# Query projection of the next head group written tile by tile between the attention heads of this group

## The chip, the cores and the metric

The kernel runs on one core of a Trainium2 chip. The metric is device time in microseconds (us) of one launch. The engines of a core work in parallel, each on its own list of instructions in order: TensorE (PE for matmuls, PEld for its weight loads), VectorE (DVE), ScalarE (ACT), GpSimd (POOL) and SyncE (SP), which issues most loads. Matmul results land in PSUM, in banks of 512 columns of 128 partitions.

## What is computed

A two-layer decoder trunk over 512 tokens of width 1024: a matrix-memory (mLSTM) layer, then a sliding-window attention layer. Each layer ends with a squared-ReLU MLP and a gated input embedding. The change lies in the attention of the second layer:

```
q = partial_rope((x @ w_q + b_q).reshape(B, S, A_Q_HEADS, A_HEAD_DIM), pos)
scores = einsum('bnqkgd,bnskd->bnkgqs', q, kb) * (A_HEAD_DIM ** -0.5)
scores = where(valid, scores, -inf)            # window of 128 tokens
m = maximum(max(scores, -1), sink)
e = exp(scores - m)
probs = e / (sum(e, -1) + exp(sink - m))
out = einsum('bnkgqs,bnskd->bnqkgd', probs, vb).reshape(B, S, D_MODEL)
return out @ w_o + b_o
```

There are 16 query heads in 4 groups; the 4 heads of a group share one key and value head. Tokens are worked in 4 tiles of 128.

## The kernel before

Every matrix product is made of three float32r matmuls (`mm3`, L87 to L90): each operand is split into a high part (a rounded copy, made by ScalarE) and a low part (the difference, made by VectorE). Weights come by DMA into `wraw`, ScalarE casts them to `whi` (L76), VectorE subtracts to `wlo` (L77); there are six buffers of each of the two.

The attention stage works on pairs of a head group `gi` (0 to 3) and a token tile `t` (0 to 3), with two functions.

`q_group(gi, t, w)` projects the queries of one group and tile: 24 matmuls of 128x256 into half a PSUM bank `mm` (two such banks; tiles 0 and 1 share one, tiles 2 and 3 the other). VectorE adds the bias and so empties the half bank (`q`, L839); POOL rotates (L786 to L789); TensorE transposes twice into the one bank `tp` (L843); ScalarE and VectorE write high and low parts into `QS` (L848, L849).

`attend(gi, t)` does the attention of the four heads of that group and tile. TensorE computes the scores in two halves of four matmuls, each half in one of three `sc` banks (L860, L861). VectorE masks (L865), takes the maximum (L866) and forms the negative maximum `anm` (L871) and the sink term `es` (L873); ScalarE takes four exponentials with their sums (L879) and that of the sink (L874); VectorE adds, inverts and scales the probabilities `pr` (L881 to L883). TensorE transposes them into a `pt` bank (L887, four transposes); ScalarE makes the high part `ah` (L891), VectorE the low part `al` (L892); for t > 0 POOL masks both into `bh` and `bl` (L899). Then 6 (t = 0) or 12 value matmuls go into another `pt` bank (two in all), and the result replaces the queries in `QS` (L910, L911).

Group 0's queries are projected ahead of the loop over the groups. The loop (L919 to L924) loads the next group's query weights, and runs `attend` and `q_group` over the four tiles. After it comes the last group's `attend`, with parts of the output projection (`wo_part`, L926 to L930) of the first two tiles between (L938). The engines' lists are not in the source's order: a scheduler sorts the instructions of the whole program by their place in the source and by its own estimate of when each could run, engine by engine. A list is then fixed; on the chip each engine follows its own.

Of the kernel before, what the change touches and what calls it, by code (L numbers as in the profile page):

```python
# [21 lines left out]
NT = S // P  # L22
# [23 lines left out]
def yoco_kernel(ctx: ExitStack, tc: tile.TileContext, A: dict, out: bass.AP):  # L46
# [18 lines left out]
    def mm_bank():  # L65
        return bank("mm")

    def tp_bank():
        return bank("tp")

    def f32(t):
        return t.bitcast(F32)
# [6 lines left out]
    def load_w(src, n, eng=V):  # L79
        raw = wpool.tile([P, 1024], F32, tag="raw", name="wraw", bufs=3)  # L80
        hi = wpool.tile([P, 1024], F32R, tag="whi", name="whi", bufs=6)
        lo = wpool.tile([P, 1024], F32R, tag="wlo", name="wlo", bufs=6)
        nc.sync.dma_start(raw[:, :n], src)
        split(raw[:, :n], n, hi[:, :n], lo[:, :n], eng)
        return hi, lo

    def mm3(o, lh, ll, rh, rl, start, stop):  # L87
        PE.matmul(o, lh, rh, start=start, stop=False)  # L88
        PE.matmul(o, lh, rl, start=False, stop=False)  # L89
        PE.matmul(o, ll, rh, start=False, stop=stop)  # L90
# [18 lines left out]
    def tsl(t):  # L109
        return slice(t * P, (t + 1) * P)  # L110
# [669 lines left out]
    def rope(x, t, nh, eng):  # L780
        tr = x[:, :, 0:ROPE].rearrange("p h (a j) -> p h a j", a=2)
        ca = cos[:, t, :].unsqueeze(1).unsqueeze(1).broadcast_to([P, nh, 2, HALF])
        sa = sin[:, t, :].unsqueeze(1).unsqueeze(1).broadcast_to([P, nh, 2, HALF])
        ta = pb.tile([P, KVH, 2, HALF], F32, tag="ta", name="ta", bufs=2)[:, :nh]
        tb = pb.tile([P, KVH, 2, HALF], F32, tag="tb", name="tb", bufs=2)[:, :nh]
        eng.tensor_mul(ta, tr, ca)  # L786
        eng.tensor_mul(tb, tr, sa)
        eng.tensor_sub(tr[:, :, 0, :], ta[:, :, 0, :], tb[:, :, 1, :])
        eng.tensor_add(tr[:, :, 1, :], ta[:, :, 1, :], tb[:, :, 0, :])  # L789
# [9 lines left out]
    w = [load_w(A["w_kv"][0, c], 1024) for c in range(4)]  # L799
# [30 lines left out]
    def q_group(gi, t, w):  # L830
        if t % 2 == 0:
            qbank[0] = mm_bank()
        ps = qbank[0][:, (t % 2) * 256:(t % 2 + 1) * 256]
        for k in range(KD):
            wh, wl = w[k // 4]
            sl = slice((k % 4) * 256, (k % 4 + 1) * 256)
            mm3(ps, XH[:, k, tsl(t)], XL[:, k, tsl(t)], wh[:, sl], wl[:, sl], k == 0, k == KD - 1)
        q = pb.tile([P, 256], F32, tag="qr", name="q", bufs=2)
        V.tensor_add(q, ps, bq[:, gi * 256:(gi + 1) * 256])  # L839
        rope(q.rearrange("p (h d) -> p h d", d=HD), t, KVH, GP)  # L840
        pt = tp_bank()
        for pr in range(2):
            PE.transpose(pt[:, tsl(pr)], q[:, tsl(pr)], ident)  # L843
        pv = pt[:, :256].rearrange("p (a s) -> p a s", a=2)
        for par in range(2):
            own, other = slice(par * HD, (par + 1) * HD), slice((1 - par) * HD, (2 - par) * HD)
            hs = slice(4 * gi + par, 4 * gi + par + 3, 2)
            ACT.copy(QS[own, hs, tsl(t)], pv[own])  # L848
            V.tensor_sub(QS[other, hs, tsl(t)], pv[own], f32(QS)[own, hs, tsl(t)])  # L849
# [63 lines left out]
    def load_q(gi):  # L913
        return [load_w(A["w_q"][gi, c], 1024) for c in range(2)]

    w = load_q(0)
    for t in range(NT):
        q_group(0, t, w)
    for gi in range(KVH - 1):  # L919
        w = load_q(gi + 1)  # L920
        for t in range(NT):
            attend(gi, t)
        for t in range(NT):
            q_group(gi + 1, t, w)  # L924

    def wo_part(ps, t, w, k0, k1):  # L926
        for k in range(k0, k1):
# [4 lines left out]
    w = [load_w(A["w_o"][0, c], 1024) for c in range(4)]  # L932
# [16 lines left out]
    for half in range(2):  # L949
        if half == 1:  # L950
            w = [load_w(A["w_o"][1, c], 1024) for c in range(4)]
# [90 lines left out]
```

## Time and profile before

| | us |
|---|---|
| runs of the kernel before (3) | 1203.20, 1203.77, 1205.82; median 1203.77 |
| the profiled execution | 1205.69 |
| its span, first to last instruction | 1204.0 |
| TensorE busy with matmuls | 1178.7 |
| VectorE busy | 879.0 |
| ScalarE busy | 587.5 |

The attention stage lies at 657 to 760 us of the span. A row of the trace gives the start of an instruction, its duration, engine, line in the kernel, operation, output and inputs, and in brackets how long the engine had been idle before and what released it. Matmuls overlap: each of 128x256 shows 0.28 us, while the next one starts 0.12 us later, so the distance of two starts tells what one costs.

### The profile page before, as it was taken

The numbers are of one execution on the slowest core, as the hardware profiler recorded it, in microseconds if no ns is written. First come the engines' busy times: TensorE is split into PE (matmuls) and PEld (weight loads), VectorE is DVE, ScalarE is ACT, GpSimd is POOL, SyncE is SP. The second block draws the span as 40 slices with busy tenths as digits, with TensorE's granted clock in tenths as the row PEclk, the third lists the DMA queues.
The fourth block names the chain that finished last, engine by engine and source line by source line (L and its number), as shares of the span: only waits on it lengthen the run. The fifth ranks groups of instructions, "written<-read, shape, count | busy, mean of one in ns | idle before, by whom it ended". The sixth has DMA issues, their size and how long they took to land. (4 is left out here: it accounts for less than half of the span.)

```text
span 1204.0 us, 15649 instructions
## 1 busy us (share of the span) xinstructions
PE 1178.7 (98%) x5918; PEld 1001.0 (83%) x5918; DVE 879.0 (73%) x1451; ACT 587.5 (49%) x1016; POOL 95.8 (8%) x189
## 2 busy tenths in 40 slices
PE   8999999999999999999999999989999999999998
PEld 7899998888888888888788998779888888888877
DVE  6555556878488589599786888596847848959974
ACT  4645552565464463464344655346645536346431
POOL 1011020100000000001201342110000000000100
PEclk9999999999999999999999999999999999999999
DMA  7322226214505306215252211361350440631511
GB/s 247 101 80 69 84 89 260 90 35 128 153 1 175 105 19 194 68 53 160 76 180 101 71 37 36 122 228 36 94 169 18 140 141 1 191 89 36 155 56 52
DMA packets 35707, 124.54 MB, mean 103 GB/s; under 512 B 4064, under 2 KB 4592, under 8 KB 35632
## 3 DMA queue, kind: packets, MB, share of 16 engines
q1 hardware_dynamic: 33552, 116.46, 30.4%
q0 software_dynamic: 2080, 7.09, 1.8%
q8 instruction: 46, 0.75, 0.2%
q14 instruction: 29, 0.24, 0.1%
HBM read 119.34 MB, written 4.19 MB: 103 GB/s over the span
## 5 line engine op out<-in xcount | busy, mean ns | idle before, releaser
L77 DVE TENSOR_TENSOR wlo<-wraw,whi 128x1024 fp32r<-128x1024 f32 (+1 forms) x168 | 204.1, 1218 | 125.2 <-ACT whi L76 124.2
L76 ACT CAST whi<-wraw 128x1024 fp32r<-128x1024 f32 (+1 forms) x168 | 173.7, 1037 | 239.6 <-PE mm L90 132.8
L88 PE MATMUL mm<-XH,whi 128*128 128x512 f32 (+1 forms) x640 | 235.1, 370 | 1.2 <-ACT ot L230 1.0
L89 PE MATMUL mm<-XL,whi 128*128 128x512 f32 (+1 forms) x640 | 235.9, 369 | 0.0
L90 PE MATMUL mm<-XH,wlo 128*128 128x512 f32 (+1 forms) x640 | 235.7, 369 | 0.0
L88 PE MATMUL mm<-whi,XH 128*128 128x512 f32 (+2 forms) x424 | 146.0, 345 | 3.9 <-DVE q L839 2.2
L89 PE MATMUL mm<-wlo,XH 128*128 128x512 f32 (+2 forms) x424 | 145.3, 343 | 0.0
L90 PE MATMUL mm<-whi,XL 128*128 128x512 f32 (+2 forms) x424 | 144.7, 343 | 0.0
L88 PEld LDWEIGHTS mm<-XH,whi 128*128 128x128 f32 x640 | 120.4, 189 | 21.8 <-ACT ot L230 1.4
L90 PEld LDWEIGHTS mm<-XH,wlo 128*128 128x128 f32 x640 | 121.1, 189 | 20.0
L89 PEld LDWEIGHTS mm<-XL,whi 128*128 128x128 f32 x640 | 121.1, 189 | 19.6
L76 ACT CAST whi<-rb 128x1024 fp32r<-128x1024 f32 x80 | 84.0, 1050 | 101.0 <-PE mm L89 56.4
L77 DVE TENSOR_TENSOR wlo<-rb,whi 128x1024 fp32r<-128x1024 f32 x80 | 97.4, 1221 | 38.9 <-ACT whi L76 38.9
L88 PEld LDWEIGHTS mm<-whi,XH 128*128 128x128 f32 x424 | 79.9, 189 | 13.0 <-DVE q L839 3.9
L89 PEld LDWEIGHTS mm<-wlo,XH 128*128 128x128 f32 x424 | 80.1, 189 | 7.7 <-issue 1.5
L90 PEld LDWEIGHTS mm<-whi,XL 128*128 128x128 f32 x424 | 80.1, 189 | 6.5 <-issue 0.8
L89 PE MATMUL mm<-wlo,S23h 128*128 128x512 f32 x128 | 50.7, 396 | 0.0
L89 PE MATMUL mm<-wlo,S4Ah 128*128 128x512 f32 x128 | 50.6, 395 | 0.0
L88 PE MATMUL mm<-whi,S23h 128*128 128x512 f32 x128 | 50.6, 395 | 0.0
L88 PE MATMUL mm<-whi,S4Ah 128*128 128x512 f32 x128 | 50.6, 395 | 0.0
L90 PE MATMUL mm<-whi,S4Al 128*128 128x512 f32 x128 | 50.3, 395 | 0.0
L633 DVE TENSOR_TENSOR res<-res,mm 128x512 f32<-128x512 f32 x72 | 48.6, 682 | 1.5 <-PE mm L90 1.0
(356 smaller groups left out, 2233.2 us busy)
## 6 DMA issues: line engine op xcount, KB each, us to landing
wraw<-in_w_up_dram SPq DMA_DIRECT2D x64, 512.0 KB, 3.9
rb<-in_w_down_dram SPq DMA_DIRECT2D x48, 512.0 KB, 4.4
wraw<-in_w_down_dram SPq DMA_DIRECT2D x16, 512.0 KB, 3.5
wraw<-in_w_gate_dram SPq DMA_DIRECT2D x16, 512.0 KB, 3.8
wraw<-in_w_vo_dram SPq DMA_DIRECT2D x19, 412.0 KB, 3.5
wraw<-in_w_qk_dram SPq DMA_DIRECT2D x8, 512.0 KB, 3.7
wraw<-in_w_out_dram SPq DMA_DIRECT2D x8, 512.0 KB, 3.9
wraw<-in_w_q_dram SPq DMA_DIRECT2D x8, 512.0 KB, 3.9
```

The costliest lines, as they stand in the source:

```text
L76: ACT.copy(hi, raw)
L77: eng.tensor_sub(lo, raw, f32(hi))
L88: PE.matmul(o, lh, rh, start=start, stop=False)
L89: PE.matmul(o, lh, rl, start=False, stop=False)
L90: PE.matmul(o, ll, rh, start=False, stop=stop)
L633: V.tensor_add(r[:, h], r[:, h], bank)
```

## The change

In the loop over the groups, `q_group(gi + 1, t, w)` is written immediately before `attend(gi, t)`, tile by tile, instead of in a loop of its own after the four tiles. Neither function is changed.

```diff
     for gi in range(KVH - 1):
         w = load_q(gi + 1)
         for t in range(NT):
+            q_group(gi + 1, t, w)
             attend(gi, t)
-        for t in range(NT):
-            q_group(gi + 1, t, w)
```

What the scheduler makes of it is seen in the engines' lists. Three places follow. The numbers in names tell buffers apart and differ between the two kernels.

Place 1: VectorE's list while the scores of group 0, tile 1 are worked on. Before, `sc_5777` is the second score half of that tile, `sc_5827` the first one of tile 2, `q_6004` the queries of group 1, tile 1.

```order
L883 TENSOR_TENSOR pr_5742<-pr_5742,sm_5743 128x512
L865 COPY_PREDICATED sc_5777<-mask_328,sc_5777 128x2x128
L866 TENSOR_REDUCE smax_5769<-sc_5777 128x2
L839 TENSOR_TENSOR q_6004<-mm_5940,bq_5268 128x256
L865 COPY_PREDICATED sc_5827<-mask_328,sc_5827 128x2x128
```

In the changed kernel the same four are `sc_5856`, `sc_5946`, `q_5833` and the probabilities `pr_5782`.

```order
L883 TENSOR_TENSOR pr_5782<-pr_5782,sm_5783 128x512
L865 COPY_PREDICATED sc_5856<-mask_328,sc_5856 128x2x128
L839 TENSOR_TENSOR q_5833<-mm_5722,bq_5268 128x256
L866 TENSOR_REDUCE smax_5848<-sc_5856 128x2
L865 COPY_PREDICATED sc_5946<-mask_328,sc_5946 128x2x128
```

The add of the queries has moved ahead of the reduction. A little later on the same list, behind the scaling of the next probabilities, the add for group 1, tile 2 stood like this before:

```order
L883 TENSOR_TENSOR pr_5789<-pr_5789,sm_5790 128x512
L865 COPY_PREDICATED sc_5834<-mask_328,sc_5834 128x2x128
L866 TENSOR_REDUCE smax_5826<-sc_5834 128x2
L911 TENSOR_TENSOR QS_5326<-pt_5760,QS_5326 128x2x128
L871 SCALAR_TENSOR_TENSOR anm_5841<-smax_5826,nsink_5270 128x4
L865 COPY_PREDICATED sc_5884<-mask_328,sc_5884 128x2x128
L839 TENSOR_TENSOR q_6044<-mm_6019,bq_5268 128x256
```

and now stands like this, with two steps between instead of five:

```order
L883 TENSOR_TENSOR pr_5868<-pr_5868,sm_5869 128x512
L911 TENSOR_TENSOR QS_5326<-pt_5800,QS_5326 128x2x128
L865 COPY_PREDICATED sc_5953<-mask_328,sc_5953 128x2x128
L839 TENSOR_TENSOR q_5930<-mm_5905,bq_5268 128x256
L849 TENSOR_TENSOR QS_5326<-tp_5755,QS_5326 64x2x128
```

Place 2: TensorE's list at the transposes of the probabilities of group 0, tile 2. Before, these are `pt_5855`; behind them come half a score half and the 24 matmuls of one projection (`mm_6407`, group 2, tile 2), and then the first value matmul, into `pt_5868`.

```order
L887 MATMUL pt_5855<-ident_66,pr_5846 128x128 x4
L860 MATMUL sc_6111<-KH_5264,QS_5326 128x256
L861 MATMUL sc_6111<-KL_5265,QS_5326 128x256
L88 MATMUL mm_6407<-whi_6099,XH_64 128x256
L89 MATMUL mm_6407<-wlo_6100,XH_64 128x256
L90 MATMUL mm_6407<-whi_6099,XL_65 128x256
```

Now the transposes are `pt_5974`, and the projection is `mm_6293`.

```order
L88 MATMUL mm_6293<-whi_6105,XH_64 128x256
L887 MATMUL pt_5974<-ident_66,pr_5965 128x128 x4
L89 MATMUL mm_6293<-wlo_6106,XH_64 128x256
L90 MATMUL mm_6293<-whi_6105,XL_65 128x256
L88 MATMUL pt_5987<-ah_5979,vo1h_5278 128x256
L843 MATMUL tp_5938<-ident_66,q_5930 128x128 x2
L89 MATMUL pt_5987<-al_5980,vo1h_5278 128x256
```

Of the projection's 24 matmuls, 22 stand ahead of the transposes now, and two between them and the first value matmul (L88, `pt_5987`).

Place 3: ScalarE's list around the exponentials of group 1, tile 2. Before, their output is `pr_6234`, from the score banks `sc_6215` and `sc_6222`; `whi_6887` and `whi_6893` are two weight tiles of the output projection, which take the buffers of group 2's query weights.

```order
L879 ACTIVATE pr_6234,sm_6235<-sc_6215,anm_6229 128x128 x2
L879 ACTIVATE pr_6234,sm_6235<-sc_6222,anm_6229 128x128 x2
L910 CAST QS_5326<-pt_6148 128x2x128
L874 ACTIVATE es_6231<-es_6231 128x4
L891 CAST ah_6191<-pt_6186 128x512
L848 CAST QS_5326<-tp_6361 64x2x128 x2
L879 ACTIVATE pr_6291,sm_6292<-sc_6272,anm_6286 128x128 x2
L879 ACTIVATE pr_6291,sm_6292<-sc_6279,anm_6286 128x128 x2
L874 ACTIVATE es_6288<-es_6288 128x4
L76 CAST whi_6887<-wraw_6886 128x1024
L910 CAST QS_5326<-pt_6199 128x2x128
L76 CAST whi_6893<-wraw_6892 128x1024
```

In the changed kernel the exponentials of that tile write `pr_6353`.

```order
L891 CAST ah_6184<-pt_6179 128x512
L848 CAST QS_5326<-tp_6143 64x2x128
L76 CAST whi_6887<-wraw_6886 128x1024
L848 CAST QS_5326<-tp_6143 64x2x128
L76 CAST whi_6893<-wraw_6892 128x1024
L879 ACTIVATE pr_6353,sm_6354<-sc_6334,anm_6348 128x128 x2
L910 CAST QS_5326<-pt_6188 128x2x128
L879 ACTIVATE pr_6353,sm_6354<-sc_6341,anm_6348 128x128 x2
```

The two casts have moved from behind the exponentials of tile 3 to ahead of those of tile 2.

## Rows read from the trace of the kernel before

**Rows 1.** The head of the page: span, busy time of each engine with its share and number of instructions.

```profile
span 1204.0 us, 15649 instructions
PE 1178.7 (98%) x5918; PEld 1001.0 (83%) x5918; DVE 879.0 (73%) x1451; ACT 587.5 (49%) x1016; POOL 95.8 (8%) x189
```

**Rows 2.** Busy time of each engine in stretches of the span (start:end and length in us, then busy us and number of instructions of PE, PEld, DVE, ACT and POOL, the granted clock, the busy share of the DMA engines and GB/s).

```profile
657.00:760.00 103.00, 96.70 (x730) 89.77 (x729) 84.68 (x224) 56.40 (x208) 32.99 (x80) 1.00 0.14 42
760.00:770.00 10.00, 10.00 (x52) 8.44 (x51) 3.08 (x8) 3.69 (x12) 2.59 (x4) 1.00 0.01 2
```

**Rows 3.** The waits of TensorE from 657 to 760 us: engine, output and line, what it waited for; us in total, times, longest.

```profile
PE mm L88 <- DVE q L839: 2.2, 4, 0.7
PE pt L89 <- DVE al L892: 1.3, 2, 0.9
PE pt L88 <- DVE QS L911: 0.5, 1, 0.5
...
PE pt L88 <- ACT ah L891: 0.4, 1, 0.4
...
PE pt L88 <- DVE al L892: 0.2, 1, 0.2
PE sc L860 <- ACT pr L879: 0.2, 1, 0.2
```

**Rows 4.** TensorE in order of time around 704 us: two projection matmuls, four transposes of probabilities and the score matmul behind them, a pair of query transposes, and two value matmuls.

```profile
703.00 0.28 PE L88 MATMUL mm<-whi,XH 128*128 128x256 f32 x1
703.12 0.28 PE L89 MATMUL mm<-wlo,XH 128*128 128x256 f32 x1
...
704.67 0.60 PE L887 MATMUL pt<-ident,pr 128*128 128x128 f32 x4
705.03 0.36 PE L860 MATMUL sc<-KH,QS 128*128 128x256 f32 x1
...
706.21 0.38 PE L88 MATMUL pt<-ah,vo0h 128*128 128x256 f32 x1
707.49 0.39 PE L89 MATMUL pt<-al,vo0h 128*128 128x256 f32 x1 [0.89 <-DVE al L892]
```

**Rows 5.** At Place 1, VectorE and TensorE in order of time.

```profile
675.28 0.42 DVE L866 TENSOR_REDUCE smax<-sc 128x2 f32<-128x256 f32 x1
675.62 0.41 DVE L839 TENSOR_TENSOR q<-mm,bq 128x256 f32<-128x256 f32 x1
...
676.09 0.39 PE L88 MATMUL mm<-whi,XH 128*128 128x256 f32 x1 [0.59 <-DVE q L839]
...
680.93 0.60 PE L887 MATMUL pt<-ident,pr 128*128 128x128 f32 x4
682.12 0.39 PE L88 MATMUL mm<-whi,XH 128*128 128x256 f32 x1 [0.59 <-DVE q L839]
```

**Rows 6.** At Place 2, TensorE, and the two steps of ScalarE and VectorE between the transposes and the value matmuls.

```profile
687.41 0.60 PE L887 MATMUL pt<-ident,pr 128*128 128x128 f32 x4
...
690.95 0.28 PE L88 MATMUL pt<-ah,vo1h 128*128 128x256 f32 x1
688.11 0.59 ACT L891 CAST ah<-pt 128x512 fp32r<-128x512 f32 x1
690.11 0.68 DVE L892 TENSOR_TENSOR al<-pt,ah 128x512 fp32r<-128x512 f32 x1
```

**Rows 7.** A projection group that waits for its bank, TensorE and VectorE (a split of weights ahead of the add).

```profile
713.26 0.28 PE L861 MATMUL sc<-KL,QS 128*128 128x256 f32 x1
714.21 0.38 PE L88 MATMUL mm<-whi,XH 128*128 128x256 f32 x1 [0.67 <-DVE q L839]
712.48 1.22 DVE L77 TENSOR_TENSOR wlo<-wraw,whi 128x1024 fp32r<-128x1024 f32 x1
```

**Rows 8.** ScalarE in order of time: four exponentials, that of the sink, and two casts of weights.

```profile
709.83 0.37 ACT L879 ACTIVATE pr<-sc,anm 128x128 f32<-128x128 f32 x1 [0.88 <-DVE anm L871]
710.18 0.36 ACT L879 ACTIVATE pr<-sc,anm 128x128 f32<-128x128 f32 x1
...
711.31 1.05 ACT L76 CAST whi<-wraw 128x1024 fp32r<-128x1024 f32 x1
...
712.51 1.07 ACT L76 CAST whi<-wraw 128x1024 fp32r<-128x1024 f32 x1
```

**Rows 9.** The instructions of TensorE between 745 and 758 us that waited.

```profile
747.62 0.36 PE L88 MATMUL pt<-ah,vo2h 128*128 128x256 f32 x1 [0.53 <-DVE QS L911]
750.59 0.41 PE L843 MATMUL tp<-ident,q 128*128 128x128 f32 x2 [0.23 <-DVE QS L849]
751.41 0.38 PE L88 MATMUL pt<-ah,vo0h 128*128 128x256 f32 x1 [0.17 <-DVE al L892]
753.02 0.36 PE L860 MATMUL sc<-KH,QS 128*128 128x256 f32 x1 [0.15 <-DVE QS L849]
755.67 0.63 PE L887 MATMUL pt<-ident,pr 128*128 128x128 f32 x4 [0.32 <-DVE es L873]
757.15 0.38 PE L88 MATMUL pt<-ah,vo0h 128*128 128x256 f32 x1 [0.36 <-ACT ah L891]
757.96 0.39 PE L89 MATMUL pt<-al,vo0h 128*128 128x256 f32 x1 [0.43 <-DVE al L892]
```

## The prediction

> **What bounds the kernel now.** I read the page first. TensorE is busy 98% of 1204.0 us, and its weight loads follow at 83% [rows 1]. So whatever an edit in the order of work can give back is idle time of TensorE, or it must avoid adding some. The change touches one stage only, the attention of the second layer, so I next took the stages one by one [rows 2]. From 657 to 760 us TensorE is busy 96.70 of 103.00 us at a granted clock of 1.00: 6.3 us idle are all that a perfect order could win there. VectorE is busy 84.68 us of the same 103, so it is nearly a second bound, and ScalarE 56.40. From 760 on TensorE is 100% busy for the next 10 us: what the stage ends earlier or later goes through to the end of the kernel, one for one.
>
> Then the waits of TensorE in that stage [rows 3]. The longest is 2.2 us in four waits of a projection group (line 88) for the VectorE add that empties its PSUM bank (`q`, L839). Next, 1.3 us for the low part of the transposed probabilities (`al`, L892), and the rest are single waits of at most 0.5 us. A wait costs somewhat more than it lists: the group at 714.21 follows a matmul begun at 713.26, 0.95 us apart, of which 0.67 is listed, 0.12 is the ordinary distance of 128x256 matmuls, and the rest is the restart [rows 4, 7].
>
> **The change, part by part.** Nothing is removed or added: the same instructions, and on SP the same loads in the same sequence. Only the order in which they are written changes, and the program's scheduler sorts them again. The lists of both kernels show that it already placed the projection groups of the next head group between the heads of this one: written last, they ran as fillers. The twelve projections start at nearly the same places of TensorE's list. So the source change works as a change of priorities, and its worth is read at the places where the lists now differ.
>
> Work per pair of a group and a token tile, from the distances of starts: 24 projection matmuls, 8 score matmuls and 12 value matmuls at 0.12 us make 5.3 us, the six transposes about 0.5 [rows 4]: 5.8 us of TensorE. VectorE spends 84.68 us of the 103 over sixteen pairs of a head group and a token tile, some 5.3 us each. Both are nearly full, so a group that is put earlier pushes another VectorE step later. That is why I expect terms of both signs.
>
> Place 1, VectorE after the first score tiles. Before, the add `q` starts at 675.62, behind the reduction that starts at 675.28, and the projection group starts at 676.09 after a listed wait of 0.59 [rows 5]. Now the add stands ahead of that reduction. It can start at 675.28, 0.34 us sooner, and the group with it. The reduction moves back by the same 0.34 us; its probabilities are wanted at 680.93, four microseconds on, so that is hidden there. At the next group the listed wait is 0.59 again (682.12). There the add stood 5 VectorE steps behind the probabilities' scaling, now it stands two behind, so I take most of the wait, 0.6 us. Together -1.0 us; the bounds are 0 (the add is held by something else) and -1.3. On POOL the rotations of the next queries (L786 to L789) now stand ahead of some masking selects (L899) that stood ahead of them; POOL is busy 32.99 of 103 us [rows 2], and the value matmuls that want the masked half come six matmuls after the first, so I give this nothing; where a rotation of some 1.3 us were in the way uncovered, that is its price, and it is inside the bounds below.
>
> Place 2, TensorE at the transposes of the third tile of group 0. Before, 24 projection matmuls lie between these transposes (687.41) and the first value matmul (690.95), and nothing waits [rows 6]. In that shadow ran the ScalarE copy `ah` (688.11, 0.59 us) and the subtraction `al` (690.11, 0.68 us). Now the 24 matmuls are mostly ahead of the transposes, and behind them stand two matmuls, one value matmul, a transpose pair and the next value matmul, which needs `al`. The cover is 0.24 + 0.12 + 0.2 = 0.6 us. The chain needs at least 0.59 + 0.68 and about 0.1 to pass on twice, 1.4 us: a new wait of 0.8 us. Where VectorE is behind, as in the case at 706.21 to 707.49, where the second value matmul came 1.28 us after the first, it is more: 0.8 and that case's 1.16 give 2.0 us as the upper bound. Between them I take 1.3, nearer to the lower end, since VectorE's list there holds two weight splits of 1.22 us but TensorE arrives later by its 24 matmuls. **+1.3 us.**
>
> Place 3, ScalarE around the exponentials of the third tile of group 1. Before, they run ahead of two casts `whi` of output weights; even those of the fourth tile do (from 709.83, casts at 711.31 and 712.51) [rows 8]. Now both casts stand ahead of them, and the second cast must wait until the last matmul of the projection group has read the old weights. The next score half needs one of three `sc` banks, and that bank is read by those exponentials. From that last matmul: 0.28 to its end, 1.05 cast, two exponentials of 0.35 and 0.2 to end, 2.2 us. TensorE has five value matmuls and four transposes there, 1.0 us. That is a wait of 1.2 us, and 0.25 more at the following half, which waits for the other pair: 1.45. The projection behind it then waits about 0.85 for its add, held by two weight splits. Before, the same stretch paid 1.16 for `al` (706.21 to 707.49, less 0.12) and 0.83 for `q` (713.26 to 714.21, less 0.12) [rows 4, 7]. Net 2.3 - 2.0 = **+0.3 us**, with bounds of -1.5 (no wait on the bank) and +2.0 (the old waits stay too).
>
> How ScalarE keeps its turn is seen at 709.83: it stood idle 0.88 us for the operand of one exponential, and what was queued behind ran afterwards in its order [rows 8]. The Trainium skill, TensorE: Matmul & The Clock Gate, section Architectural detail: the array is 16× 32×32, not 1× 128×128, says that the queues of ScalarE and VectorE are strictly first in, first out. By it the waiting cast holds the exponentials and Place 3 stands as above; were it otherwise, its 1.45 would be 0 and the sum 1.4 us lower. The trace agrees with the rule.
>
> The tail, the last four tiles. No projections are left to fill. The listed waits between 747 and 758 us are 2.2 us in seven pieces [rows 9], about 3.5 with the restarts. Counted in the lists at the distances above, more matmuls lie between the scores and the transposes of the last tiles (6.0 us instead of 4.2 in one, 6.2 instead of 5.6 in another) and between the query transposes and the scores (4.9 and 2.6 us instead of 2.0 and 1.4). That takes away the waits of 0.23, 0.15, 0.32 and part of 0.43, with restarts some 1.6 us. Against it, the transposes of the last tile of group 2 now have no matmul at all between them and their first value matmul (1.2 us before), and the tile before it has 1.8 instead of 5.0: +1.1. **-0.5 us**, bounds -2 and +2. The pre-computed output products (L938) are the same number, moved a little earlier.
>
> Sum: -1.0 + 1.3 + 0.3 - 0.5 = +0.1 us. The profiled execution took 1205.69 us, the changed one would take 1205.8 by the same measure. It lies 1.9 us above the median of 1203.77, inside the runs shown (1203.2 to 1205.82). I carry the sum over to the median: **1203.9 us**.
>
> **The rivals.** A difference of under 0.2% (2.4 us) can hardly be told from no change here.
>
> Nothing happens: the scheduler evens it all out, the waits merely change their names. For it: the near equal lists. It gives 1203.8, and cannot be told by time from my forecast.
>
> Slower: the three score banks become the pace. Because the next queries are ready sooner, score matmuls are listed further ahead of the values of older tiles; each new half then waits for exponentials three halves back, which wait for VectorE's `anm`. Against it: scores waited on exponentials only 0.2 us in one wait before [rows 3]. For it: the new list puts scores of two tiles ahead of many transposes. At Place 3's price of 1.45 us a tile, four further tiles without the offset give +5.8, 1209.6 us; two such tiles (2.9 us) decide it. The Trainium skill, Perfetto Trace Analysis, Optimization Strategy, says that a gap which keeps repeating on the engine that should be saturated can mean too little PSUM for the next tile; by this rule the time would be that 1209.6. No row of the trace before shows such a repeating gap, so it does not decide yet.
>
> Faster: the four waits for `q` go altogether (2.2 listed and about 0.75 of restarts), the tail gives its 1.6, and Place 2 costs its lower bound: -2.9 - 1.6 + 0.8 = -3.7, 1200.1 us. For it: at Place 1 the add clearly moves forward. Against it: VectorE is at 82% of the stage and its sum of work is the same.
>
> **How the numbers follow.** My forecast, terms that cancel, 0.36; nothing happens 0.20; slower by the banks 0.24; faster 0.20. The first two are both within 0.2%, so same is 0.56. The likeliest's own range is 1201.4 to 1206.3. All bounds together would reach from -4.0 to +6.0; I give 1200.2 to 1208.6, which takes in the faster case's near half and the slower one's, and leaves about 2 in 10 out.
>
> **What would show it.** In the changed profile: waits of line 88 for `q` (L839) fall from 2.2 to about 1.3 us; waits of the value matmuls (L88, L89) for `ah` and `al` rise from 1.9 to about 3; waits of line 860 for L879, 0.2 before, rise above 1 us. Idle time of TensorE in the stage stays between 4 and 9 us, and its stage ends within 2.4 us of before. It is wrong if line 860 waits for L879 in more than three tiles (slower), or if the sum of TensorE's waits in the stage falls under 3 us (faster), or if a later stage changes its time on its own, since I give that nothing.

## The result

The changed kernel takes a little longer: 1208.09 us in the median (1205.70 to 1208.67) against 1204.61 for the kernel before on the same chip. The ratio, estimated from all runs and not from the two medians alone, is 1.0021 with a 95% interval of 1.0011 to 1.0031. A second comparison of the same two kernels, below, gave 1.0015 (1.0006 to 1.0024): some 2 us, small, but both intervals lie above 1. The median lies inside the forecast range (1200.2 to 1208.6), 0.5 us under its upper end; the forecast itself was 1203.9.

The head of the page of the changed kernel, and two stretches of it, which answer to [rows 1, 2]:

```profile
span 1206.4 us, 15646 instructions
PE 1180.2 (98%) x5918; PEld 1002.5 (83%) x5918; DVE 879.5 (73%) x1451; ACT 588.6 (49%) x1016; POOL 95.0 (8%) x189
```

```profile
657.00:760.00 103.00, 94.83 (x715) 87.63 (x714) 85.45 (x225) 57.79 (x213) 31.80 (x80) 1.00 0.13 42
760.00:770.00 10.00, 10.00 (x58) 8.65 (x57) 2.71 (x7) 2.63 (x5) 1.27 (x2) 1.00 0.01 2
```

The span is 2.4 us longer. In the attention stage TensorE now stands idle 8.2 us of 103 instead of 6.3. Its waits there changed their names, as forecast; these rows answer to [rows 3]:

```profile
PE pt L89 <- DVE al L892: 2.4, 4, 0.8
PE sc L860 <- ACT pr L879: 1.7, 3, 0.9
PE pt L88 <- ACT ah L891: 1.5, 2, 1.0
PE tp L843 <- DVE QS L849: 0.7, 1, 0.7
PE mm L88 <- DVE q L839: 0.6, 2, 0.3
PE mm L88 <- ACT QS L910: 0.5, 1, 0.5
```

The waits for the projection's add `q` fell from 2.2 to 0.6 us. Those for `ah` and `al` rose from 1.9 to 3.9, and the scores' wait for the exponentials from 0.2 to 1.7.

**Place 1** answers to [rows 5]. VectorE's add now stands ahead of the reduction, and TensorE's group follows 0.78 and 0.62 us after the transposes instead of 1.25 (from 674.84) and 1.19; no wait is listed any more. The two places, in order of time:

```profile
674.22 0.66 PE L887 MATMUL pt<-ident,pr 128*128 128x128 f32 x4
674.53 0.42 DVE L839 TENSOR_TENSOR q<-mm,bq 128x256 f32<-128x256 f32 x1
674.87 0.41 DVE L866 TENSOR_REDUCE smax<-sc 128x2 f32<-128x256 f32 x1
...
675.00 0.39 PE L88 MATMUL mm<-whi,XH 128*128 128x256 f32 x1
...
679.86 0.60 PE L887 MATMUL pt<-ident,pr 128*128 128x128 f32 x4
680.48 0.39 PE L88 MATMUL mm<-whi,XH 128*128 128x256 f32 x1
```

**Place 2** answers to [rows 6]. Two matmuls stand between the transposes and the value matmuls, which wait twice:

```profile
688.66 0.60 PE L887 MATMUL pt<-ident,pr 128*128 128x128 f32 x4
...
689.99 0.39 PE L88 MATMUL pt<-ah,vo1h 128*128 128x256 f32 x1 [0.49 <-ACT ah L891]
690.22 0.38 PE L843 MATMUL tp<-ident,q 128*128 128x128 f32 x2
691.43 0.39 PE L89 MATMUL pt<-al,vo1h 128*128 128x256 f32 x1 [0.84 <-DVE al L892]
```

**Place 3** answers to [rows 7, 8]. ScalarE's two casts stand ahead of the exponentials, the first of them waits for the projection's matmuls, and the scores wait for their bank:

```profile
706.22 1.05 ACT L76 CAST whi<-wraw 128x1024 fp32r<-128x1024 f32 x1 [1.27 <-PE mm L90]
707.76 1.05 ACT L76 CAST whi<-wraw 128x1024 fp32r<-128x1024 f32 x1
708.84 0.37 ACT L879 ACTIVATE pr<-sc,anm 128x128 f32<-128x128 f32 x1
...
709.70 0.39 PE L860 MATMUL sc<-KH,QS 128*128 128x256 f32 x1 [0.94 <-ACT pr L879]
```

**The tail** answers to [rows 9]. Seven waits again, but 4.0 us listed instead of 2.2:

```profile
742.02 0.41 PE L843 MATMUL tp<-ident,q 128*128 128x128 f32 x2 [0.67 <-DVE QS L849]
746.20 0.39 PE L89 MATMUL pt<-al,vo1h 128*128 128x256 f32 x1 [0.66 <-DVE al L892]
750.38 0.38 PE L88 MATMUL pt<-ah,vo2h 128*128 128x256 f32 x1 [1.01 <-ACT ah L891]
751.09 0.39 PE L860 MATMUL sc<-KH,QS 128*128 128x256 f32 x1 [0.33 <-ACT pr L879]
754.62 0.39 PE L860 MATMUL sc<-KH,QS 128*128 128x256 f32 x1 [0.47 <-ACT pr L879]
756.54 0.50 PE L88 MATMUL mm<-whi,QS 128*128 128x512 f32 x1 [0.46 <-ACT QS L910]
759.23 0.38 PE L89 MATMUL pt<-al,vo0h 128*128 128x256 f32 x1 [0.41 <-DVE al L892]
```

**Behind the stage** something changed that the prediction gave nothing for. In the layer norm that follows, three waits of TensorE stand close together, and then the 128x256 matmuls start 0.21 us apart instead of 0.12:

```profile
801.74 0.38 PE L88 MATMUL mm<-XH,whi 128*128 128x256 f32 x1 [0.24 <-ACT XH L133]
802.91 0.62 PE L88 MATMUL mm<-XH,whi 128*128 128x256 f32 x3 [0.79 <-DVE res L157]
805.33 1.29 PE L129 MATMUL tp<-ident,res 128*128 128x128 f32 x8 [1.80 <-DVE res L146]
...
806.85 0.41 PE L88 MATMUL mm<-XH,whi 128*128 128x256 f32 x1
807.06 0.41 PE L89 MATMUL mm<-XL,whi 128*128 128x256 f32 x1
```

The same five microseconds in both kernels, the changed one first; the number behind the engines is the granted clock:

```profile
805.00:810.00 5.00, 4.67 (x26) 4.58 (x27) 5.00 (x11) 2.13 (x3) 0.00 (x0) 0.66 0.57 144
```

```profile
805.00:810.00 5.00, 5.00 (x44) 5.00 (x43) 4.82 (x8) 2.75 (x5) 1.23 (x1) 1.00 0.64 206
```

For a part of that window, 3.41 us from 806.25, TensorE was granted the lower of its two levels (1.2 GHz of 2.4); below this is called a half-clock stretch. And the scheduler's lists differ here too. In TensorE's list the kernel before has the third group of transposes in two halves with four projection matmuls between them:

```profile
802.18 0.63 PE L129 MATMUL tp<-ident,res 128*128 128x128 f32 x4 [1.50 <-DVE res L146]
802.57 0.75 PE L88 MATMUL mm<-XH,whi 128*128 128x256 f32 x4
...
804.42 0.66 PE L129 MATMUL tp<-ident,res 128*128 128x128 f32 x4 [1.11 <-DVE XL L134]
```

The changed kernel has those four first and then all eight transposes. The prediction went by the lists inside the attention stage only.

### The profile page after: what moved, and what is told of

It is laid out like the page before. It is cut to its first block, busy times and chain, and to the rows that moved or that the text cites. A ratio compares the mean times of both kernels' runs of the same rounds, so it can differ in the third digit from the quotient of the medians.

```text
span 1206.4 us, 15646 instructions
## 1 busy us (share of the span) xinstructions
PE 1180.2 (98%) x5918; PEld 1002.5 (83%) x5918; DVE 879.5 (73%) x1451; ACT 588.6 (49%) x1016; POOL 95.0 (8%) x189
## 4 chain that ended last, share of the span: by engine, by line
PE 89%; DVE 6%; ACT 2%; DMA 2%; issue 1%; SPq 0%; DVEq 0%; ACTq 0%
PE mm L90 27%; PE mm L89 27%; PE mm L88 27%; DVE wlo L77 1%; PE tp L129 1%; DMA res<-spill 1%; ACT pr L879 1%; DMA xraw<-in_xT_dram 1%; PE tp L88 1%; PE tp L89 1%; PE tp L90 1%; ACT whi L76 1%; DVE sc L865 1%; DVE QS L849 1%; PE mm L260 0%
## 5 line engine op out<-in xcount | busy, mean ns | idle before, releaser
L88 PE MATMUL mm<-XH,whi 128*128 128x512 f32 (+1 forms) x640 | 235.4, 370 | 1.3 <-DVE res L157 0.8
L88 PE MATMUL mm<-whi,XH 128*128 128x512 f32 (+2 forms) x424 | 146.1, 345 | 2.3 <-ACT XH L133 1.1
L88 PEld LDWEIGHTS mm<-XH,whi 128*128 128x128 f32 x640 | 120.6, 189 | 21.7 <-DVE res L157 1.0
L88 PEld LDWEIGHTS mm<-whi,XH 128*128 128x128 f32 x424 | 80.0, 189 | 10.9 <-ACT XH L133 2.5
L88 PE MATMUL mm<-whi,S23h 128*128 128x512 f32 x128 | 50.6, 395 | 0.0
L88 PE MATMUL mm<-whi,S4Ah 128*128 128x512 f32 x128 | 50.6, 395 | 0.0
```

## The experiments

To move one thing at a time, the runs below (all but the first and the one with exchanged lines) write every engine's list out by hand: each instruction is ordered behind the one that precedes it in the wanted list, without a semaphore. The source is that of the changed kernel.

```
ins = TAG[key + "." + str(j)]
if last is not None:
    tc.add_manual_dep(ins, last.name, mybir.DependencyInfo(mybir.DependencyClass.NoSync, ...))
last = ins
```

The measure is taken between three instructions of TensorE that have the same work between them in every kernel, but for one matmul of 0.12 us, the twelve of the filler, and the last row of the table: the first score matmul (L860), the first transpose of the second layer norm group (L129), and the first matmul on A11h, the next projection. The start of the stage itself differs by up to 3.2 us from trace to trace (662.3 to 665.5), with nothing changed ahead of it, so spans say less. A part of that is the clock: the four traces with a half-clock stretch near 227 us start the stage last (664.55 to 665.54), the eight without any stretch ahead of it at 662.32 to 664.03. The three rows in the run with the lists of before through the attention and of the changed kernel behind it:

```profile
664.12 0.28 PE L860 MATMUL sc<-KH,QS 128*128 128x256 f32 x1
...
797.98 0.38 PE L129 MATMUL tp<-ident,res 128*128 128x128 f32 x2
...
849.92 0.40 PE L88 MATMUL mm<-whi,A11h 128*128 128x512 f32 x1
```

That is 133.86 and 51.94 us. All runs, each kernel's traces read in this way (the waits of one list in the attention repeat from trace to trace within 0.03 us):

| lists through the attention | lists behind it | to L129, us | on to A11h, us | lowest granted clock in 5 us, 800 to 815 us | ratio to before, 95% |
|---|---|---|---|---|---|
| before | before | 134.79 | 51.29 | 1.00 | 1 |
| changed | changed | 136.12 | 52.58 | 0.66 | 1.0021 (1.0011, 1.0031) |
| changed, again | changed | 136.14 | 52.10 | 0.66 | 1.0015 (1.0006, 1.0024) |
| changed | before | 137.26 | 53.19 | 0.50 | 1.0022 (1.0013, 1.0032) |
| before | changed | 133.86 | 51.94 | 0.71 | 0.9996 (0.9987, 1.0005) |
| changed, Place 2 undone | changed | 135.95 | 51.91 | 0.66 | one run |
| changed, Place 3 undone | changed | 140.48 | 51.90 | 0.66 | one run |
| changed, Place 3 again | changed | 138.61 | 52.82 | 0.75 | one run |
| changed, then before's tail | changed | 137.70 | 51.86 | 0.74 | one run |
| changed, splits on GpSimd | changed | 139.22 | 50.40 | 1.00 | one run |
| before with Place 1 | changed | 134.98 | 50.40 | 1.00 | 0.9996 (0.9985, 1.0006) |
| before | changed, with filler | 133.92 | 50.40 | 1.00 | 0.9990 (0.9981, 0.9999) |
| changed | changed, with filler | 136.22 | 50.40 | 1.00 | 1.0005 (0.9996, 1.0014) |
| lines exchanged, as sorted | as sorted | 138.21 | 50.24 | 1.00 | 1.0028 (1.0018, 1.0038) |

Four of the sums to L129 hold a half-clock stretch of their own, of 3.41 us, which costs some 1.5 us (the last section has the working): both runs of Place 3 (at 715.78 and 720.34 us), the splits on GpSimd (711.33) and the lines exchanged (784.60). The others hold none.

**The changed kernel again.** No edit.

> The changed kernel once more. In its first trace the span was 1206.4 us against 1204.0, and by landmarks the difference is -0.5 at the first score matmul (664.35 against 664.85), about +1.5 at the first transposes of the next layer norm (796.11 against 794.12, less the early start), and about +1.4 behind them, where three waits of TensorE between 801.74 and 805.33 were followed by 128x256 matmuls 0.21 us apart instead of 0.12 (granted clock 0.66 in 805 to 810 us). Theory 'the half-clock stretch belongs to this order': it stands at the same place again, granted clock near 0.66 in that window, span 1206 to 1207, ratio to before 1.001 to 1.003. Rival 'the half-clock stretch fell there by chance': the same window at 1.00 and the span 1204.5 to 1205.3, with the stage still 1.5 us later.

The half-clock stretch stood at the same place again (0.66), the stage took 136.14 us, and the ratio was 1.0015. That speaks for the first theory, but the next run takes half of it back.

**The two halves of the difference.**

```
 lists of TensorE, VectorE, ScalarE, GpSimd
- those of the changed kernel, throughout
+ those of the changed kernel up to the last instruction of attend(3, 3)
+ those of the kernel before behind it
```

> The scheduler's lists differ not only in the attention stage but also behind it: in the layer norm that follows and in the last one. Here every engine's list is written out by hand: that of the changed kernel up to its last instruction of the attention, that of the kernel before behind it. Theory 'the stage and what stands behind it each cost about 1.5': first layer norm transposes 1.5 to 2 us later than before (about 796), no half-clock stretch, the span about 1.0 to 1.5 over before, ratio 1.001. Theory 'all of the loss is the stage, the layer norm follows by itself': ratio 1.002, half-clock stretch as in the changed kernel. Theory 'the loss is behind the stage': span within 0.5 of before, ratio 1.000.

```
+ those of the kernel before up to the last instruction of attend(3, 3)
+ those of the changed kernel behind it
```

> The opposite: every engine's list of the kernel before up to the last instruction of the attention, and that of the changed kernel behind it (layer norm, and the last layer norm). Theory 'each costs about 1.5': the stage ends as before (first layer norm transposes near 794.1), then three waits close together, a half-clock stretch near 804 to 808, span 1.4 over before, ratio 1.001. Theory 'all is the stage': as before, ratio 1.000, no half-clock stretch. Theory 'all is behind the stage': ratio 1.002.

The two agree with each other and with none of the theories as they were put. With the same lists behind, the changed stage costs 136.13 - 133.86 = 2.3 us, or 137.26 - 134.79 = 2.5; the ratios say the same (1.0015 against 0.9996, 1.0022 against 1). So at least the whole loss is the stage. What the scheduler changed behind it is a gain in the traces: 0.9 to 1.1 us ahead of the second transposes, where TensorE waits less for the residual that comes back by DMA (`res`, L157), and 0.9 behind them where the clock holds (50.40 against 51.29). From A11h to the end it loses 0.2 again (353.3 against 353.06 us). And the half-clock stretch belongs to neither order alone: it stood behind before's order too, and longer (0.50).

**Place 2 undone.**

```
 TensorE
+L887 pt<-ident,pr x4         (probabilities of group 0, tile 2)
 L88..L90 mm<-whi,XH ... x24  (projection of group 2, tile 2; two of them were behind the transposes)
-L887 pt<-ident,pr x4
```

> All lists written out as the changed kernel has them; on TensorE alone the four transposes of the probabilities of group 0, tile 2 stand again ahead of the 24 projection matmuls of group 2, tile 2, as before the change. Measured by the time from the first score matmul (L860) to the second group of layer norm transposes (L129): 136.1 us in the changed kernel. Prediction's mechanism (lost cover): the waits for ah and al there, 1.65 us with restarts, go, and all of it arrives: 134.5. Rival 'VectorE is late there anyway': al still comes behind the two steps that hold it, one wait moves to another place, 135.5 or more. Rival 'later waits eat it': the two waits go, 136.1.

It gave 135.95 us: 0.2 came back of the 1.65 that Place 2 costs by its rows. The rival that VectorE is late there anyway holds. With 24 matmuls of cover the wait for `ah` went, but the one for `al` stayed (0.48 us listed instead of 0.84), and two new ones came ahead of it, for `pr` (0.15) and for `QS` (0.18). The two rows of ScalarE show one reason. The copy `ah`, which `al` needs, was queued behind a query copy that itself waited 2.14 us for VectorE:

```profile
687.86 0.37 ACT L848 CAST QS<-tp 64x256 fp32r<-64x256 f32 x1 [2.14 <-DVE QS L849]
688.25 0.59 ACT L891 CAST ah<-pt 128x512 fp32r<-128x512 f32 x1
```

**Place 3 undone, twice.** First the casts of two weight chunks behind the exponentials, with their subtractions on VectorE one and seven steps later:

```
 ScalarE
-L76 whi ; L848 QS ; L76 whi ; L879 pr x4 (group 1, tile 2)
+L848 QS x2 ; L879 pr x4 ; L76 whi ; ... ; L76 whi
```

> All lists as the changed kernel has them; on ScalarE the two casts whi of output weights stand behind the exponentials of group 1, tile 2, and of the query copies, and their subtractions on VectorE a few steps later. Prediction's mechanism: the wait of L860 for L879 (0.94 listed at 708.16) goes; the old waits for al and q, 2.0 us, do not come back since TensorE's list stays: 136.1 - 1.1 to -1.9 = 134.2 to 135.0 us. Rival 'the bank is paced by anm on VectorE, not by the casts': the wait stays within 0.3 us of 1.12, 136.0.

Then with the subtractions moved as far back, behind the scaling of the probabilities (L883):

> The run with Place 3 undone took 140.48 us from the first score matmul to the second group of layer norm transposes instead of 136.1: in its trace VectorE's subtraction wlo stood at its old place and waited for the cast that had been moved back, and with it the step es (L873) that ScalarE and, through the query copies, TensorE waited for (2.51 us). Here the two subtractions are moved back with their casts, behind the scaling of the probabilities; all else is the changed kernel's lists. If Place 3 is a cost of its own: the wait of L860 for L879 (1.12 with restart) is gone and the sum is 134.7 to 135.3. If it is only a matter of which step is late: waits of about 1 us come up under other names, 135.8 to 136.5.

The wait for the score bank went as forecast, from 1.12 us with its restart to 0.30. But in both runs a longer one came: 2.5 us for `QS`, and the totals were 140.48 and 138.61. Some 1.5 us of each is the half-clock stretch that followed this wait 1.5 to 1.7 us later; the other 2.8 and 1.0 us over the changed kernel are waits. In the first, VectorE's subtraction waited 2.38 us for the moved cast and held `es` (L873), which held ScalarE's `es` and the query copy behind it. In the second, a subtraction stood ahead of the finishing step of an older tile on VectorE, and TensorE waited for that:

```profile
716.41 1.65 DVE L77 TENSOR_TENSOR wlo<-wraw,whi 128x1024 fp32r<-128x1024 f32 x1
718.09 0.42 DVE L911 TENSOR_TENSOR QS<-pt,QS 128x256 fp32r<-128x256 f32 x1
...
718.66 0.36 PE L88 MATMUL pt<-ah,vo1h 128*128 128x256 f32 x1 [2.50 <-DVE QS L911]
```

Neither theory foresaw a worse total; the rival's "under other names" is nearer. So these two runs do not price Place 3.

**The tail of before.**

```
 all four lists
 as the changed kernel up to 725.9 us of its trace
-its own remainder of the attention
+what is left of the attention, in the order of the kernel before
```

> The changed kernel's lists up to 725.9 us of its trace; from there to the end of the attention each engine takes what is left in the order of the kernel before; behind it the changed kernel's lists. In the tail the waits of the changed kernel come to 5.3 us with restarts between 741 and 759, those of before to 3.8. Theory 'the tail's order costs 1.5': 136.1 - 1.5 = 134.6 us. Rival 'the tail's waits follow from what the head leaves late on VectorE': about as much waiting under other names, 135.8 to 136.5.

The waits between 750 and 761 us became those of [rows 9], 3.8 us with restarts instead of 5.3. But two new ones came where the two lists meet, 1.72 and 0.74 us listed, and the sum was 137.70, 1.6 more than the changed kernel. That is worse than both theories; whether the tail's order costs 1.5 us by itself is not settled by it, since the seam is of my making.

**Place 1 alone.**

```
 VectorE, lists of before
+L839 q   (group 1, tile 1)
 L866 smax<-sc
-L839 q
 (and q of group 1, tile 2, three places of VectorE's list earlier)
```

> The lists of the kernel before through the attention and of the changed kernel behind it, as in the run with the lists behind alone (133.86 us from the first score matmul to the second group of layer norm transposes), and one part of the change: the two adds q (L839) of group 1, tiles 1 and 2, stand earlier on VectorE (ahead of the reduction of group 0, tile 1; ahead of a finishing step of tile 0). Prediction's mechanism: two waits of L88 for q shrink by 0.83 us together, and it all arrives: 133.0, time about 0.8 us under that of the lists behind alone, some 1.5 us under before (ratio 0.9985 to 0.9993). Rival 'what is pushed back on VectorE comes late': al or q later by the same, 133.9, ratio 0.9996.

The two waits shrank by 0.9 us, nearly as in the changed kernel (1.0), and the stage took 134.98, 1.1 more than without the edit: the rival, and more. TensorE came earlier to its next projection, whose add stands behind a weight split on VectorE, and waited there for what it had saved:

```profile
683.13 1.22 DVE L77 TENSOR_TENSOR wlo<-wraw,whi 128x1024 fp32r<-128x1024 f32 x1
...
685.19 0.42 DVE L839 TENSOR_TENSOR q<-mm,bq 128x256 f32<-128x256 f32 x1
...
685.66 0.39 PE L88 MATMUL mm<-whi,XH 128*128 128x256 f32 x1 [0.84 <-DVE q L839]
```

Without the edit that group did not wait.

**Weight splits on GpSimd.**

```
-    w = [load_w(A["w_o"][0, c], 1024) for c in range(4)]
+    w = [load_w(A["w_o"][0, c], 1024, GP) for c in range(4)]
     (and the first two chunks of w_o[1])
```

> The changed kernel's lists, but the six subtractions wlo (L77, 1.22 us each) of output weights that VectorE does inside the stage (two near 684, two near 708, two near 735 us) are done by GpSimd at the same places in time. It takes 7.3 us of VectorE's 85 away and moves nothing else. Theory 'TensorE's waits in this stage are VectorE coming late, one step behind another in its list, and not the cover on TensorE': the waits for al, q and QS near 690, 711 and 717, and 741 to 749 shrink, 136.1 becomes 133.0 to 135.0. Rival 'the waits are set by TensorE's order (cover) alone': 135.8 to 136.3. Where GpSimd's subtraction takes so long that masked values (L899) come late, it is more than 136.5.

It took 139.22 us. GpSimd needs twice as long for a split; the second row is the granted clock behind the longest wait of this run (1.96 us, for the exponentials, at 710.21):

```profile
L77 POOL TENSOR_TENSOR wlo<-wraw,whi 128x1024 fp32r<-128x1024 f32 x5 | 12.3, 2476 | 5.2 <-ACT whi L76 5.2
```

```profile
712.00:716.00 4.00, 3.98 (x23) 3.55 (x23) 3.91 (x13) 1.19 (x7) 1.96 (x6) 0.66 0.50 147
```

TensorE then waited 0.6 us for a masked half (`bl`, L899), as the last sentence of the expectation has it, but also 3.7 instead of 1.7 us for the exponentials, while the waits for `al` fell from 2.4 to 1.4 (counted to 765 us, since this run's stage ends later) and those for `q` from 0.6 to 0.3. So VectorE's list is part of what makes `al` and `q` late, and this run cannot price it, the less as the half-clock stretch is in its sum. The Trainium skill, GPSIMD Engine Reference, section 4.1 Engine selection, gives GpSimd about twice VectorE's time for elementwise work on two inputs; 2.48 against 1.22 us agrees.

**Filler matmuls in the layer norm.** Twelve matmuls into the bank that the third group of transposes overwrites right afterwards, first with the lists of before through the attention, then with the changed kernel's throughout. They are extra work; nothing is left out.

```
             pt = tp_bank()
+            for j in range(fill if b == 0 else 0):
+                FILL.append(PE.matmul(pt[:, :256], XH[:, 0, tsl(0)], XH[:, 0, :256], start=True, stop=True))
```

> The lists of the kernel before through the attention, those of the changed kernel behind it, and 12 extra 128x256 matmuls (1.44 us at 0.12) on TensorE ahead of the third group of layer norm transposes, into the bank that these overwrite, so the output stays. Without them TensorE waited there 2.3 us with restart and the granted clock was at its half for a stretch right behind (0.71 in 800 to 805 us). Theory 'the half-clock stretch comes from the idle time there': the clock stays at 1.00 from 795 to 815, from the second group of transposes to the first matmul of the next projection (A11h) 50.4 us instead of 51.9, median 1 to 1.5 under that of the lists without filler, 1.5 to 2 under before, ratio 0.998 to 0.9990. Rival 'idle time there has no part in it': stretch as often as before, ratio 0.9996.

> The changed kernel's lists throughout, with the same 12 extra matmuls ahead of the third group of layer norm transposes. Without them the changed kernel took 136.13 us from the first score matmul to the second group of layer norm transposes and 52.1 to 52.6 from there to A11h, with a half-clock stretch in both traces. If its loss is the stage (+2.3), less what its order behind the stage wins where the clock holds (-0.9), and the rest is the half-clock stretch: 136.1 and 50.4 us, clock 1.00 from 795 to 815, ratio to before 1.0000 to 1.0008. Rival 'the half-clock stretch is no part of what the medians differ by': ratio as without filler, 1.0015 to 1.0021.

Clock and landmarks came out as the first theory has it in both. The lines of the helper are four or two further down here (the filler is L129, the transposes L131, `res` L150):

```profile
798.74 1.10 PE L88 MATMUL mm<-XH,whi 128*128 128x256 f32 x4 [0.24 <-ACT XH L135]
799.68 1.60 PE L129 MATMUL tp<-XH 128*128 128x256 f32 x12
801.55 0.66 PE L131 MATMUL tp<-ident,res 128*128 128x128 f32 x4 [0.28 <-DVE res L150]
```

The transposes waited 0.28 instead of 1.80 us, the granted clock stayed at 1.00 from 795 to 815 us in both traces, and 50.40 us passed to A11h instead of 51.9 to 52.6. With the filler the changed kernel stands at 1.0005 of before instead of 1.0015 to 1.0021, and before's stage with the changed kernel's order behind it at 0.9990 instead of 0.9996. That last step is 0.7 us, where 1 to 1.5 were expected, and its two intervals overlap. It is the only kernel here whose interval lies under 1 (0.9981 to 0.9999), a gain of some 1.2 us on before.

The mean granted clock of each of these runs is known too, and says how far the traces speak for the medians. It was 0.9989 over the 11 runs of that kernel and 0.9982 over the 18 of before beside them: an estimated 0.8 us (0.0007 of 1204) of the 1.2. But without filler it was 0.9977 over 11 runs of the changed kernel and 0.9977 over the 26 of before beside them. So half-clock stretches cost both kernels about the same on the whole, and by these runs the loss of the changed kernel is not the clock's. They do make the scatter: of those 26, the runs at 0.999 took 1202.92 to 1204.58 us, those at 0.997 or less 1205.28 to 1208.02.

**The two lines exchanged.**

```
         for t in range(NT):
-            q_group(gi + 1, t, w)
             attend(gi, t)
+            q_group(gi + 1, t, w)
```

> The source with the two lines in the loop exchanged: attend(gi, t) first, then q_group(gi + 1, t, w); the scheduler sorts as it likes. The lists then differ from those of the changed kernel and of before in some 800 places of TensorE. Theory 'the cost is that queries take precedence over the heads of the same tile': 134 to 135.5 us between the same two points, ratio 0.999 to 1.001. Rival 'any other order of the source sorts the stage worse than the one the kernel was left with': 136 or more, ratio 1.001 or more.

The numbers are the rival's: 138.21 us and 1.0028. But the place is another. One wait of 3.3 us, 3.46 with its restart, stands behind the stage, for the residual's addition (L157), and a half-clock stretch follows it:

```profile
783.65 0.50 PE L88 MATMUL mm<-whi,QS 128*128 128x512 f32 x1 [3.29 <-DVE res L157]
```

```profile
784.00:788.00 4.00, 4.00 (x12) 3.14 (x11) 4.00 (x8) 0.00 (x0) 0.67 (x1) 0.57 1.03 420
```

The 138.21 also holds less work than the other sums: nine matmuls of 128x512 (2.1 us at 0.23) stand behind L129 here. The last value matmul of the attention is a better mark. It starts 110.70 us after the first score matmul, 110.16 before and 112.85 in the changed kernel. Ahead of it stand three matmuls of 128x512 fewer than before here, and four more in the changed kernel, so I estimate a loss inside the attention of 1.2 us for this order and 1.8 for the changed one. The rest of this run's loss lies at the residual and its stretch. A third place for the same lines, and the time moves at a third point of the program.

## Why the prediction came out as it did

The range held and the sign of the loss was among its cases, but it is a sum of terms of which two came out with the other sign and one was missing. That the median fell inside owes more to the range's width of 8.4 us than to the sum: the stage was put at +0.1 us and cost 2.3, and what came behind it was not in the sum at all. The wait with its restart is read as in the prediction, from the distance of two starts less the usual one (1.21 us from 690.22 to 691.43, less 0.2 behind a transpose pair, is 1.0).

| step | predicted, us | in the trace, us |
|---|---|---|
| Place 1, the add `q` earlier | -1.0 | (0.78 - 1.25) + (0.62 - 1.19) = -1.0 |
| Place 2, lost cover | +1.3 | 0.65 + 1.00 = +1.65 |
| Place 3, casts ahead of exponentials | +0.3 | 1.12 + 0.45 - 1.16 - 0.83 = -0.4 |
| two further waits between 717 and 720 us | none | 0.77 - 0.33 = +0.4 |
| the tail | -0.5 | 5.29 - 3.83 = +1.5 |
| the stage | +0.1 | +2.3 |
| behind the stage | 0 | -0.9 to -1.1 ahead of the second transposes, -0.9 behind them, +0.2 behind A11h; in the trace back about +1.5 where the clock falls |

**Right.** Places 1, 2 and 3 lie inside their bounds and Places 1 and 2 within 0.4 us. The markers came: the waits for `q` fell (to 0.6, further than the 1.3 expected), those for `ah` and `al` rose past 3, L860 waited for L879 over 1 us but in three tiles only, and TensorE idled 8.2 us. The stage ends 2.3 to 2.5 us later with the same lists behind it, at the limit of the 2.4 given. The lost cover that was priced at the tail came too: the last tile of group 2, with no matmul between its transposes and its values, waited 1.19 us with its restart instead of 0.69, and the tile before it 0.81 instead of nothing: +1.3 where 1.1 was put.

**Mis-sized, with the wrong sign: the tail.** The prediction let the new order of the tail take waits away ("some 1.6 us") and charged it with nothing but lost cover. Waits did go, even more of them: 0.23, 0.15 and 0.32 went, and three others, 2.5 us with restarts; the 0.43 stayed (0.41). (The 3.5 us of the prediction for all of them leaves out one of 0.15 at 748.13 us; with it and the restarts they are 3.83.) The step that failed is that nothing was put for new waits of the scores and queries that now run further ahead. Two tiles waited for a score bank (0.59 and 0.63 with restarts) and two steps waited for `QS` (0.82 and 0.62), together 2.7 us. The first is the rival of the score banks on a small scale: it came in the tail, at 0.6 us a tile instead of 1.45.

**Missing: the lists behind the stage.** "The change touches one stage only" is true of the source and false of the program. The scheduler sorts all of it, and 147 places of TensorE's list outside the attention differ as well, in the two layer norms and what lies around them. The prediction named a later stage that changes on its own as what would make it wrong; the traces show that it does, with a gain that nearly pays for the stage (-1.8 where the clock holds, +0.2 behind A11h). In the trace of the changed kernel a half-clock stretch takes most of that back, but by the recorded clocks the kernel before pays as much for such stretches, at this place or another.

**The price of a place is not what undoing it gives.** The terms nearly add up in the trace (2.1 by the places, 2.3 between the landmarks), and yet no place gave its price back: -0.2 for 1.65 at Place 2, +2.8 and +1.0 at Place 3 (without the half-clock stretches), and Place 1 alone, -0.9 by its two waits, cost 1.1. Each engine runs its list in order, and the four lists fit each other; a step moved in one of them is held by the step ahead of it, or holds the next. What the sum of the places describes is where the time shows, not which edit would win it.

**Open.** Whether the tail's order or what reaches it late makes its 1.5 us. And how much of the gain behind the stage holds over many runs: with equal clocks these terms leave a loss of some 0.7 us, and the medians gave 1.8 and 2.5. The -0.9 behind the second transposes rests on one trace of the kernel before. The one other trace with its order there has a half-clock stretch of 6.83 us, and the filler was not tried on that order.

## What to carry to other kernels

Where a scheduler places the instructions, compare its lists to the end of the program, not only around the edit: a moved line is sorted into other stages too, and here these won back, in the traces, most of what the stage lost. Where several engines are nearly full, a wait's price is no promise of what removing it brings; test the whole list, and expect the wait to come back one step further on. A short stretch of work that costs nothing, put in TensorE's longest wait, can be worth as much as a better order: here 1.5 us in a trace, and 0.7 to 1.9 us by the ratios.

## What the runs showed of the hardware

A half-clock stretch followed a wait of TensorE of 1.8 us in seven of nine traces with the changed order behind the stage, and also waits of 2.0 us (splits on GpSimd) and 2.5 us (both runs of Place 3) inside the stage and of 3.3 us behind it (lines exchanged). In two of the nine it did not come, with the same wait of 1.8 us, and none followed a wait of 1.7 us inside the stage (tail of before, at 729.01). The stretch costs about 1.5 us (51.9 instead of 50.40 us to A11h, with the same waits; the sums up to 52.8 also hold a longer wait for the residual), since the matmuls in it start 0.21 instead of 0.12 us apart. One such stretch is nearly as large as the whole difference between the two kernels, though over all runs both kernels show the same mean clock, 0.9977. With the filler, TensorE's longest wait there was 0.28 us and no such stretch came in either trace.
